# First layer's attention: scores and transposes in larger and fewer rows, group 2's factor multiplied into its probabilities

## The chip, the cores and the metric

The kernel runs on one core of a Trainium2 chip. The core has a matrix engine (TensorE, PE in the profile; its weight loads are listed as PEld), VectorE (DVE), ScalarE (ACT), GpSimd (POOL) and SyncE (SP), which mostly issues transfers. Matrix products land in PSUM, eight banks of 512 float32 columns by 128 partitions; VectorE and ScalarE read them from there. The metric is the device time of one execution in microseconds.

## What is computed

A decoder trunk of two layers over a residual stream of 512 positions by 1024 features. The change concerns the attention of the first layer, cut here to what matters:

```python
A_GROUPS = ((128, 1), (512, 4), (2048, 16))      # (window, dilation), four heads of 64 each

def dilated_mixer(xn, w_qkv, w_o, cos, sin):
    q, k, v = jnp.split(xn @ w_qkv, 3, axis=-1)   # q, k get a partial rotation
    for g, (window, r) in enumerate(A_GROUPS):
        # positions gathered by dilation r, banded causal attention in each class
        o, lse = banded_attention(gather(q), gather(k), gather(v), window // r)
        outs.append(o)
        lses.append(lse)
    alpha = jax.nn.softmax(jnp.stack(lses, axis=0), axis=0)      # weight of each group
    o = jnp.concatenate([outs[g] * alpha[g][..., None] for g in range(3)], axis=2)
    return o.reshape(B, T, A_WIDTH) @ w_o
```

The weight alpha of a group depends on the softmax denominators of all three groups, so it is known only when the last group's scores are done. After the attention come the output product with w_o, a normalisation, a feed-forward part, and the second layer.

## The kernel before

The order of all instructions is written out by hand; each engine works through its own queue in that order, and the framework adds the waits between engines. Matrix products that need precision are made as three products of high and low halves (`mm3`, L283 to L285), so every weight is first copied to a high half on ScalarE (L60, L64) and its low half made on VectorE (L78, L82). `W.get()` hands out weights and keeps some pieces ahead.

The first layer's attention is laid around three wide projections, each a call of `wide_proj`: queries and keys of group 1, those of group 2 (both `qk_ps`), and the values of groups 1 and 2 (`v_ps`). Group 0's projections come before. A `wide_proj` holds four PSUM banks, one for each block of 128 positions, through four steps; a step is 24 matmuls on TensorE. After each step it runs a list of small work (a "row" in the text) and then one step of the generator `down0`, which prepares sums of the feed-forward's weights: loads and stores on SP's queue and four subtractions on VectorE (`down_sums`, L586 to L589). `sums` is another such generator. The four lists of a call are given to it in `between`.

The small work for group g and block b:

- `qk_transpose` (L1109, `qkT_ps`): four transposes on TensorE into one bank, copied out by VectorE (L1112).
- `scores` (L1134 for group 0, L1136 for the others, `s_ps`): for each half of the heads, hh = 0 and 1, two products. The two halves use the upper and the lower 64 rows of the array, and each half has a bank of its own. In groups 1 and 2 a block's scores for two heads fill half a bank. `softmax` then reads each head's scores from PSUM on VectorE (L1119, with a second record that reads the accumulator) and exponentiates on ScalarE (L1120).
- `p_transpose` (L1156, `pT_ps`): the probabilities transposed on TensorE, copied out by ScalarE (L1158). Group 0 has two banks of them for a block, the others one.
- `factors` (L1180 to L1191): the weights alpha, with the softmax denominators in them, as a chain of small VectorE instructions and one ScalarE exponential, spread to 64 columns a head as `fac`, by VectorE for group 0 and POOL for the others.

After the third projection come, for each group and pair of heads `pr`: `pv` (L1205, L1208, `o_ps`), the product of probabilities and values, copied to SBUF by ScalarE (L1211, L1213; groups 1 and 2 back into the order of positions on the way); `weigh` (L1221, `f_ps`), the factors transposed by four transposes on TensorE and multiplied onto it by VectorE (L1223); `combine` (L1229, L1230), high and low halves of the result. Group 2's `combine` runs in `late`, a hook between the second and the third block of the output product (`Proj.finish`), together with transposes of the convolution's columns (`cv_ps`, L566) and of gains (`g_ps`, L1414). The output product (`acc`) opens two banks for each of its four blocks.

PSUM banks, and buffers of the pool `t2` (eight of 2 KB a partition, which hold probabilities, `ow` and the convolution's rows among others), are given out again when their last reader in program order is through.

Of the kernel before, what the change touches and what calls it, by code (L numbers as in the profile page):

```python
# [9 lines left out]
F32 = mybir.dt.float32  # L10
# [3 lines left out]
ALU = mybir.AluOpType  # L14
# [103 lines left out]
def trunk_kernel(ctx, tc, x, norm_gains, w_qkv_a, w_o_a, w_q_b, w_o_b, kv_norm, w_kvf, b_f,  # L118
                 w_up, conv_w, conv_b, w_down, rope, out):
    nc = tc.nc  # L120
    act, dve, pool, pe, sp = nc.scalar, nc.vector, nc.gpsimd, nc.tensor, nc.sync
# [8 lines left out]
    def t8(shape, dt=F32, name="t8"):  # L130
        return p8.tile(shape, dt, tag="t8", name=name)

    def t4(shape, dt=F32, name="t4"):
        return p4.tile(shape, dt, tag="t4", name=name)

    def t2(shape, dt=F32, name="t2"):
        return p2.tile(shape, dt, tag="t2", name=name)

    def bank(shape, name="bank"):
        return psp.tile(shape, F32, tag="ps", name=name)  # L140
# [81 lines left out]
    h = cst.tile([128, NB, D], F32, name="h")  # L222
# [889 lines left out]
        dve.tensor_copy(qkT[g][:, b], o)  # L1112

    P = {}

    def softmax(g, b, hd, s, mask, p):

        keep = st[:, g, b] if g else st0[:, b]
        dve.tensor_tensor_reduce(p, s, mask, -0.125, BIG, ALU.add, ALU.min, keep[:, hd:hd + 1])  # L1119
        act.activation(p, p, AF.Exp, bias=keep[:, hd:hd + 1], scale=-1.0, accum_out=keep[:, 4 + hd:5 + hd])  # L1120

    def scores(g, b):
        q = qkT[g]

        k0 = 0 if (g == 0 and b) else 1
        n = 256 if g == 0 else 128
        p = None
        for hh in range(2):
            hs_ = slice(64 * hh, 64 * hh + 64)
            o = bank([128, 2, n], name="s_ps")  # L1130
            for pr in range(2):
                if g == 0:
                    ov = o[:, pr, k0 * 128:].rearrange("p (k c) -> p k c", c=128)
                    pe.matmul(ov, q[hs_, b, pr, :], q[hs_, b - 1 + k0:b + 1, 2 + pr, :], start=True, stop=True)  # L1134
                else:
                    pe.matmul(o[:, pr, :], q[hs_, b, pr, :], q[hs_, b, 2 + pr, :], start=True, stop=True)  # L1136
            if g == 0 or hh == 0:
                p = t2([128, 512 // n, n], name="p")
                P[g, b, hh] = p
            for pr in range(2):  # L1140
                if g == 0:
                    softmax(g, b, 2 * pr + hh, o[:, pr, k0 * 128:], mask0[:, k0 * 128:], p[:, pr, k0 * 128:])
                else:
                    softmax(g, b, 2 * pr + hh, o[:, pr, :], mask0[:, 128:256] if g == 1 else mask2,
                            p[:, 2 * hh + pr, :])

    def p_transpose(g, b):
        if b == 0:
            PT[g] = [t8([128, 4, 4, 128], name=f"PT{g}_{i}") for i in range(2 if g == 0 else 1)]
        for pr in range(len(PT[g])):  # L1150
            p = P.pop((g, b, pr))
            o = bank([128, 4, 128], name="pT_ps")
            js = [0, 1, 2, 3] if (g or b) else [1, 3]
            pf = p.rearrange("p a c -> p (a c)")
            for j in js:
                pe.transpose(o[:, j, :], pf[:, j * 128:(j + 1) * 128], ident)  # L1156
            if len(js) == 4:
                act.copy(PT[g][pr][:, b], o)  # L1158
            else:
                for j in js:  # L1160
                    act.copy(PT[g][pr][:, b, j], o[:, j, :])
# [12 lines left out]
    def factors():  # L1174

        m, l = st[:, :, :, 0:4], st[:, :, :, 4:8]
        mn = sml.tile([128, 4, 4], F32, tag="f_mn", name="f_mn", bufs=1)
        f = sml.tile([128, 3, 4, 4], F32, tag="f_f", name="f_f", bufs=1)
        w = sml.tile([128, 3, 4, 4], F32, tag="f_w", name="f_w", bufs=1)
        dve.tensor_tensor(mn, m[:, 0], m[:, 1], ALU.min)  # L1180
        dve.tensor_tensor(mn, mn, m[:, 2], ALU.min)
        dve.tensor_tensor(f, mn[:, None].to_broadcast([128, 3, 4, 4]), m, ALU.subtract)
        act.activation(f, f, AF.Exp)
        dve.tensor_tensor(w, l, f, ALU.mult)
        dve.tensor_tensor(mn, w[:, 0], w[:, 1], ALU.add)
        dve.tensor_tensor(mn, mn, w[:, 2], ALU.add)
        dve.reciprocal(mn, mn)
        dve.tensor_tensor(f, f, mn[:, None].to_broadcast([128, 3, 4, 4]), ALU.mult)
        for g in range(3):
            fac[g] = t4([128, 4, 4, HD], name="fac")  # L1190
            (pool.tensor_copy if g else dve.tensor_copy)(fac[g], f[:, g, :, :, None].to_broadcast([128, 4, 4, HD]))  # L1191

    ow = {}

    def pv(g, pr):
        o = bank([128, T], name="o_ps")
        for b in range(4):
            for hh in range(2):
                hd = 2 * pr + hh
                ov = o[64 * hh:64 * hh + 64, b * 128:(b + 1) * 128]  # L1200
                vs = slice(hd * 64, hd * 64 + 64)
                if g == 0:
                    ks = [0, 1] if b else [1]
                    for k in ks:
                        pe.matmul(ov, V[g][:, b - 1 + k, vs], PT[g][hh][:, b, 2 * pr + k, :],  # L1205
                                  start=k == ks[0], stop=k == 1)
                else:
                    pe.matmul(ov, V[g][:, b, vs], PT[g][0][:, b, 2 * hh + pr, :], start=True, stop=True)  # L1208
        ow[g, pr] = t = t2([128, T], name="ow")
        if g == 0:  # L1210
            act.copy(t, o)  # L1211
        else:
            act.copy(t.rearrange("p (l r) -> p r l", r=4), o.rearrange("p (r l) -> p r l", r=4))  # L1213

    OT = {}

    def weigh(g, pr):

        fb = bank([128, 4, 128], name="f_ps")
        for r in range(4):  # L1220
            pe.transpose(fb[:, r, :], fac[g][:, r, 2 * pr:2 * pr + 2, :].rearrange("p h d -> p (h d)"), ident)  # L1221
        t = ow[g, pr].rearrange("p (l r) -> p r l", r=4)
        dve.tensor_tensor(t, t, fb, ALU.mult)  # L1223

    def combine(g, pr):
        t = ow.pop((g, pr))
        if pr == 0:
            OT[g] = t8([128, 2, 2, T], F32R, name=f"OT{g}")
        act.copy(OT[g][:, 0, pr, :], t)  # L1229
        dve.tensor_tensor(OT[g][:, 1, pr, :], t, OT[g][:, 0, pr, :].bitcast(F32), ALU.subtract)  # L1230

    def v_proj0(between):
        banks = []
# [20 lines left out]
    L = later  # L1254
# [86 lines left out]
    sums = down_sums([(1, 6), (1, 7)], in_two, sp, 1, 3)  # L1341
# [18 lines left out]
    def v_post(g, b, o):  # L1360
        if b == 0:
            for i in (1, 2):
# [4 lines left out]
    down0 = down_sums([*[(0, j) for j in range(ND)], (1, 8)], in_one, sp, 1, 1)  # L1367
    v_proj0([[L(qk_transpose, 0, 0), L(qk_transpose, 0, 1), L(next, down0)],
             [L(qk_transpose, 0, 2), L(qk_transpose, 0, 3), L(scores, 0, 0), L(scores, 0, 1), L(next, sums), L(next, down0)]])
    wide_proj(1, "qk_ps", qk_post, [  # L1370
        [L(p_transpose, 0, 0)],
        [L(scores, 0, 2), L(scores, 0, 3), L(p_transpose, 0, 1), L(next, sums)],
        [L(p_transpose, 0, 2), L(next, sums)],
        [stat_out, L(p_transpose, 0, 3), L(next, sums)]])
    wide_proj(2, "qk_ps", qk_post, [
        [L(qk_transpose, 1, 0), L(qk_transpose, 1, 1), L(next, sums)],
        [L(qk_transpose, 1, 2), L(scores, 1, 0), L(scores, 1, 1)],
        [L(qk_transpose, 1, 3), L(p_transpose, 1, 0)],
        [L(scores, 1, 2), L(scores, 1, 3), L(p_transpose, 1, 1), stat_in]])
    W.ahead = 3  # L1380
    wide_proj(1, "v_ps", v_post, [
        [L(qk_transpose, 2, 0), L(qk_transpose, 2, 1), L(p_transpose, 1, 2)],
        [L(qk_transpose, 2, 2), L(qk_transpose, 2, 3), L(scores, 2, 0), L(scores, 2, 1), L(p_transpose, 1, 3)],
        [L(scores, 2, 2), L(scores, 2, 3), L(p_transpose, 2, 0)],
        [factors, L(p_transpose, 2, 1), L(p_transpose, 2, 2), L(p_transpose, 2, 3)]])
    for g in range(2):
        for pr in range(2):
            pv(g, pr)
    weigh(0, 0)
    weigh(0, 1)  # L1390
    combine(0, 0)
    pv(2, 0)
    pv(2, 1)
    weigh(1, 0)
    combine(0, 1)
    weigh(1, 1)
    combine(1, 0)
    weigh(2, 0)
    combine(1, 1)
    weigh(2, 1)  # L1400

    rows = load_conv(0)
    grow = t2([16, 128], name="g_rows")
# [414 lines left out]
```

## Time and profile before

| | |
|---|---|
| median of 3 runs | 1103.44 us (1103.12 to 1103.47) |
| profiled execution | 1106.61 us, of which 1104.8 us are the span of the profile |
| first layer's attention, from the first transposes of group 0 to the output product | 41.65 to 145.34 us of the span |
| TensorE's granted clock | 0.998 of full speed |

The profile records one execution. A line of a timeline begins with an instruction's start and its duration in microseconds, then the engine, the line of the kernel, the operation, output and inputs by the program's names, and their shapes; equal neighbours are merged and counted (x8). In brackets stands how long the engine had been idle before and what released it. A line that groups instructions has, after the count, the sum of their time in microseconds and the mean of one in nanoseconds. TensorE's matmuls overlap, so what a group costs is read from start to start, not from its duration.

### The profile page before, as it was taken

How to read it: one execution, taken by the hardware profiler on the slowest of the kernel's cores; microseconds unless marked ns; L12 is line 12 of the kernel's file. 1: busy time of each engine (PE TensorE's matmuls, PEld its weight loads, DVE VectorE, ACT ScalarE, POOL GpSimd, SP SyncE). 2: the span in 40 equal slices, each digit the busy share in tenths (PEclk: the TensorE clock that was granted, in tenths of full speed). 3: DMA queues.
4: the chain of work that ended last, by engine and by line, in shares of the span. 5: the costliest groups of instructions: out<-in, count | busy, mean ns of one | idle time of the engine just before them, and what ended most of it. 6: DMA issues, size and time to landing. Idle time of an engine off the chain costs nothing.

```text
span 1104.8 us, 18091 instructions
## 1 busy us (share of the span) xinstructions
PE 1095.3 (99%) x6605; PEld 952.5 (86%) x6605; DVE 874.6 (79%) x1497; ACT 671.5 (61%) x1115; POOL 171.5 (16%) x245
## 2 busy tenths in 40 slices
PE   8999999999999999999999999999999999999997
PEld 6988889999999988888878888889899999988886
DVE  5697778887787779898587676868888788779894
ACT  6754566556665647576552488746656666647573
POOL 1723000411111211000000211100311111211000
PEclk9999999999999999999999999999999999999999
DMA  9699864378888979885445767784368888989862
GB/s 319 142 366 408 337 191 124 75 184 211 188 192 193 231 256 326 325 289 149 133 153 206 273 183 198 234 269 131 83 178 201 198 188 188 233 268 318 318 248 77
DMA packets 191554, 242.67 MB, mean 220 GB/s; under 512 B 12784, under 2 KB 138728, under 8 KB 191464
## 3 DMA queue, kind: packets, MB, share of 16 engines
q1 hardware_dynamic: 175848, 189.33, 52.8%
q0 software_dynamic: 14944, 52.18, 20.6%
q8 instruction: 52, 0.85, 0.3%
q14 instruction: 38, 0.31, 0.1%
q10 hardware_dynamic: 672, 0.00, 0.0%
HBM read 172.37 MB, written 39.73 MB: 192 GB/s over the span
## 4 chain that ended last, share of the span: by engine, by line
PE 98%; DMA 1%; DVE 0%; issue 0%; SPq 0%; ACT 0%; DVEq 0%
PE up L283 13%; PE up L284 13%; PE up L285 13%; PE acc L283 9%; PE acc L285 9%; PE acc L284 8%; PE v_ps L285 2%; PE v_ps L283 2%; PE v_ps L284 2%; PE qk_ps L284 2%; PE qk_ps L285 2%; PE qk_ps L283 2%; PE pT_ps L1659 2%; PE o_ps L1674 2%; PE s_ps L1625 2%; PE first L285 1%
## 5 line engine op out<-in xcount | busy, mean ns | idle before, releaser
L283 PE MATMUL acc<-w 128*128 128x512 f32 (+1 forms) x311 | 120.6, 388 | 0.3 <-DVE mix L332 0.3
L285 PE MATMUL acc<-w 128*128 128x512 f32 (+1 forms) x311 | 120.4, 387 | 0.0
L284 PE MATMUL acc<-w 128*128 128x512 f32 (+1 forms) x267 | 103.2, 387 | 0.0
L283 PE MATMUL up<-xsh,w 128*128 128x256 f32 x352 | 99.6, 283 | 0.0
L284 PE MATMUL up<-xsl,w 128*128 128x256 f32 x352 | 99.6, 283 | 0.0
L285 PE MATMUL up<-xsh,w 128*128 128x256 f32 x352 | 99.6, 283 | 0.0
L78 DVE TENSOR_TENSOR w<-wraw,w 128x1024 fp32r<-128x1024 f32 x62 | 82.4, 1349 | 21.7 <-ACT w L60 17.4
L620 ACT ACTIVATE bb<-up,conv 128x512 f32<-128x512 f32 x80 | 59.7, 776 | 58.4 <-DVE up L1007 47.6
L60 ACT CAST w<-wraw 128x1024 fp32r<-128x1024 f32 x81 | 83.3, 1049 | 17.0 <-PE v_ps L284 6.9
L284 PE MATMUL up<-xcl,w 128*128 128x512 f32 (+1 forms) x276 | 93.5, 339 | 0.0
L284 PE MATMUL up<-xbl,w 128*128 128x512 f32 (+1 forms) x276 | 93.5, 339 | 0.0
L285 PE MATMUL up<-xch,w 128*128 128x512 f32 (+1 forms) x276 | 93.5, 339 | 0.0
L283 PE MATMUL up<-xbh,w 128*128 128x512 f32 (+1 forms) x276 | 93.5, 339 | 0.0
L283 PE MATMUL up<-xch,w 128*128 128x512 f32 (+1 forms) x276 | 93.5, 339 | 0.0
L285 PE MATMUL up<-xbh,w 128*128 128x512 f32 (+1 forms) x276 | 93.4, 338 | 0.0
L283 PEld LDWEIGHTS acc<-w 128*128 128x128 f32 x311 | 58.4, 188 | 12.3 <-DVE mix L332 0.7
L285 PEld LDWEIGHTS acc<-w 128*128 128x128 f32 x311 | 58.4, 188 | 12.0
L283 PEld LDWEIGHTS up<-xsh,w 128*128 128x128 f32 x352 | 67.6, 192 | 0.0
L284 PEld LDWEIGHTS up<-xsl,w 128*128 128x128 f32 x352 | 67.6, 192 | 0.0
L285 PEld LDWEIGHTS up<-xsh,w 128*128 128x128 f32 x352 | 67.6, 192 | 0.0
L621 DVE SCALAR_TENSOR_TENSOR bb<-up,conv,bb 128x511 f32<-128x511 f32 x80 | 59.5, 744 | 5.8 <-ACT bb L620 5.7
L623 DVE SCALAR_TENSOR_TENSOR bb<-up,conv,bb 128x510 f32<-128x510 f32 x80 | 59.9, 749 | 2.8
(310 smaller groups left out, 3112.0 us busy)
## 6 DMA issues: line engine op xcount, KB each, us to landing
wraw<-in_w_up_dram SPq DMA_DIRECT2D x88, 512.0 KB
w<-wraw POOLq DMA_DIRECT2D x32, 512.0 KB, 6.4
dT<-dsums SPq DMA_DIRECT2D x28, 512.0 KB
w<-wsum POOLq DMA_DIRECT2D x24, 512.0 KB, 5.7
dsums<-in_w_down_dram SPq DMA_DIRECT2D x22, 512.0 KB
dsums<-in_w_down_dram SPq DMA_DIRECT2D x44, 256.0 KB
hD<-hc POOLq DMA_DIRECT2D x44, 256.0 KB, 7.1
dact<-hD SPq DMA_DIRECT2D x44, 256.0 KB
```

The source lines that it names most:

```text
L60: (copy or self.nc.scalar.copy)(pair[:, 0], raw)
L78: self.nc.vector.tensor_tensor(pair[:, 1], raw, pair[:, 0].bitcast(F32), ALU.subtract)
L283: pe.matmul(o, ah, bh, start=first, stop=False, skip_group_check=shared)
L284: pe.matmul(o, ah, bl, start=False, stop=False, skip_group_check=shared)
L285: pe.matmul(o, al, bh, start=False, stop=last, skip_group_check=shared)
L620: act.activation(bb[:, s, :], ps, AF.Identity, bias=cp[:, 3, ch:ch + 1], scale=cp[:, 2, ch:ch + 1])
L621: dve.scalar_tensor_tensor(bb[:, s, 1:], ps[:, :T - 1], cp[:, 1, ch:ch + 1], bb[:, s, 1:], ALU.mult, ALU.add)
L623: dve.scalar_tensor_tensor(bb[:, s, 2:], ps[:, :T - 2], cp[:, 0, ch:ch + 1], bb[:, s, 2:], ALU.mult, ALU.add)
L1625: pe.matmul(sc[j, i][hh][:, :nn], qT[j][own, qp, i * 128:(i + 1) * 128], k[own, kp, :nn], start=qp + kp == 0, stop=qp == 1)
L1659: pe.transpose(o[:, k0 + k, :], p[:, hh, k * 128:(k + 1) * 128], ident)
L1674: pe.matmul(o[64 * hh:64 * hh + 64, i * 128:(i + 1) * 128], Vt[hd // 8][:, k, (hd % 8) * 64:(hd % 8) * 64 + 64], pT[j, i, hh][:, k, :], st ...
```

## The change

Four things change in the first layer's attention.

1. In groups 1 and 2 the scores of blocks b and b + 1 (b even) share the two banks that one block used: one bank for each half of the heads, with block b in its first half and block b + 1 in its second.
2. The lists between the steps are cut differently: the two blocks of a pair have their transposes in one list, and the last list of each projection is left with none.
3. `factors` moves from the last list of the third projection to the one before, behind one step of `down0` (the generator has no step more, so a later one falls away). Group 2's factors are multiplied onto its probabilities before these are transposed, two blocks on VectorE and two on POOL; they are no longer spread, transposed and multiplied onto the outputs. Group 2's probabilities are transposed behind the first two `pv`.
4. Group 2's `pv` leaves its output in PSUM, and `combine` takes it from there, back into the order of positions on the way.

```diff
     P = {}
+    s_banks = {}
...
-            o = bank([128, 2, n], name="s_ps")
+            if g == 0:
+                o = bank([128, 2, n], name="s_ps")
+            else:
+                if b % 2 == 0:
+                    s_banks[hh] = bank([128, 2, 2, n], name="s_ps")
+                o = s_banks[hh][:, b % 2]
...
-        for g in range(3):
+        for b in range(4):
+            p = P[2, b, 0].rearrange("p (h r) c -> p h r c", h=2)
+            fb = f[:, 2, b].rearrange("p (r h) -> p h r", h=2)[:, :, :, None].to_broadcast([128, 2, 2, 128])
+            (pool if b >= 2 else dve).tensor_tensor(p, p, fb, ALU.mult)
+        for g in range(2):
             fac[g] = t4([128, 4, 4, HD], name="fac")
             (pool.tensor_copy if g else dve.tensor_copy)(fac[g], f[:, g, :, :, None].to_broadcast([128, 4, 4, HD]))
...
+        if g == 2:
+            ow[g, pr] = o
+            return
         ow[g, pr] = t = t2([128, T], name="ow")
...
-        act.copy(OT[g][:, 0, pr, :], t)
-        dve.tensor_tensor(OT[g][:, 1, pr, :], t, OT[g][:, 0, pr, :].bitcast(F32), ALU.subtract)
+        hi, lo = (OT[g][:, part, pr, :] for part in range(2))
+        if g == 2:
+            t = t.rearrange("p (r l) -> p r l", r=4)
+            hi, lo = (a.rearrange("p (l r) -> p r l", r=4) for a in (hi, lo))
+        act.copy(hi, t)
+        dve.tensor_tensor(lo, t, hi.bitcast(F32), ALU.subtract)
...
     wide_proj(1, "qk_ps", qk_post, [
-        [L(p_transpose, 0, 0)],
-        [L(scores, 0, 2), L(scores, 0, 3), L(p_transpose, 0, 1), L(next, sums)],
-        [L(p_transpose, 0, 2), L(next, sums)],
-        [stat_out, L(p_transpose, 0, 3), L(next, sums)]])
+        [L(p_transpose, 0, 0), L(p_transpose, 0, 1)],
+        [L(scores, 0, 2), L(scores, 0, 3), L(next, sums)],
+        [L(p_transpose, 0, 2), L(p_transpose, 0, 3), L(next, sums)],
+        [stat_out, L(next, sums)]])
     wide_proj(2, "qk_ps", qk_post, [
         [L(qk_transpose, 1, 0), L(qk_transpose, 1, 1), L(next, sums)],
-        [L(qk_transpose, 1, 2), L(scores, 1, 0), L(scores, 1, 1)],
-        [L(qk_transpose, 1, 3), L(p_transpose, 1, 0)],
-        [L(scores, 1, 2), L(scores, 1, 3), L(p_transpose, 1, 1), stat_in]])
+        [L(qk_transpose, 1, 2), L(qk_transpose, 1, 3), L(scores, 1, 0), L(scores, 1, 1)],
+        [L(p_transpose, 1, 0), L(p_transpose, 1, 1), L(scores, 1, 2), L(scores, 1, 3)],
+        [stat_in]])
     W.ahead = 3
     wide_proj(1, "v_ps", v_post, [
-        [L(qk_transpose, 2, 0), L(qk_transpose, 2, 1), L(p_transpose, 1, 2)],
-        [L(qk_transpose, 2, 2), L(qk_transpose, 2, 3), L(scores, 2, 0), L(scores, 2, 1), L(p_transpose, 1, 3)],
-        [L(scores, 2, 2), L(scores, 2, 3), L(p_transpose, 2, 0)],
-        [factors, L(p_transpose, 2, 1), L(p_transpose, 2, 2), L(p_transpose, 2, 3)]])
-    for g in range(2):
-        for pr in range(2):
-            pv(g, pr)
+        [L(p_transpose, 1, 2), L(p_transpose, 1, 3), L(qk_transpose, 2, 0), L(qk_transpose, 2, 1)],
+        [L(qk_transpose, 2, 2), L(qk_transpose, 2, 3), L(scores, 2, 0), L(scores, 2, 1)],
+        [L(scores, 2, 2), L(scores, 2, 3), L(next, down0, None), factors],
+        []])
+    pv(0, 0)
+    pv(0, 1)
+    for b in range(4):
+        p_transpose(2, b)
+    pv(1, 0)
+    pv(1, 1)
     weigh(0, 0)
     weigh(0, 1)
     combine(0, 0)
-    pv(2, 0)
-    pv(2, 1)
     weigh(1, 0)
     combine(0, 1)
     weigh(1, 1)
+    pv(2, 0)
+    pv(2, 1)
     combine(1, 0)
-    weigh(2, 0)
     combine(1, 1)
-    weigh(2, 1)
```

## The prediction

> **What bounds the kernel now.** I read the page first, then TensorE's timeline through the first layer's attention, then VectorE's beside it.
>
> ```profile
> span 1104.8 us, 18091 instructions
> PE 1095.3 (99%) x6605; PEld 952.5 (86%) x6605; DVE 874.6 (79%) x1497; ACT 671.5 (61%) x1115; POOL 171.5 (16%) x245
> ...
> PE 98%; DMA 1%; DVE 0%; issue 0%; SPq 0%; ACT 0%; DVEq 0%
> ```
>
> TensorE is busy for 99% of the span and makes 98% of the chain that ended last. A change here is worth what it takes from TensorE's queue or puts into it as waiting; work on other engines counts only where TensorE waits for it. So each row of small instructions between projections is priced by TensorE's start times (first column, us; "x8" is eight merged instructions).
>
> ```profile
> 71.19 1.03 PE L1156 MATMUL pT_ps<-ident,p 128*128 128x128 f32 x8
> 71.98 0.48 PE L283 MATMUL qk_ps<-w,xph 128*128 128x512 f32 x1
> ...
> 104.24 1.26 PE L1136 MATMUL s_ps<-qkT 64*128 64x128 f32 x16
> 105.43 0.66 PE L1156 MATMUL pT_ps<-ident,p 128*128 128x128 f32 x4
> ```
>
> Eight transposes take 71.98 - 71.19 = 0.79 us. The scores of two blocks (16 records) take 105.43 - 104.24 = 1.19 us when nothing holds them. Against these the other rows show waits:
>
> ```profile
> 64.54 1.32 PE L1156 MATMUL pT_ps<-ident,p 128*128 128x128 f32 x8
> 65.61 0.47 PE L283 MATMUL qk_ps<-w,xph 128*128 128x512 f32 x1
> ...
> 90.73 1.56 PE L1136 MATMUL s_ps<-qkT 64*128 64x128 f32 x16
> 92.22 0.50 PE L283 MATMUL qk_ps<-w,xph 128*128 128x512 f32 x1
> ...
> 119.19 1.72 PE L1136 MATMUL s_ps<-qkT 64*128 64x128 f32 x16
> 120.84 0.66 PE L1156 MATMUL pT_ps<-ident,p 128*128 128x128 f32 x4
> ...
> 126.91 1.26 PE L1136 MATMUL s_ps<-qkT 64*128 64x128 f32 x16
> 128.33 0.66 PE L1156 MATMUL pT_ps<-ident,p 128*128 128x128 f32 x4 [0.16 <-DVE st L1119]
> ```
>
> Transposes at 64.54: 1.07, so 0.28 of waiting. Scores: 1.49, 1.65 and 1.42, so 0.30, 0.46 and 0.23. The cause is banks: the projection holds four of the eight, and four for two blocks of scores with one or two for transposes in the same row ask for five or six.
>
> **What is removed.** Group 2's factors are no longer transposed: 8 of 24 transposes.
>
> ```profile
> 134.29 1.47 PE L1156 MATMUL pT_ps<-ident,p 128*128 128x128 f32 x12
> 135.69 3.33 PE L1205 MATMUL o_ps<-PT,V 128*64 128x128 f32 x56
> 138.80 1.97 PE L1208 MATMUL o_ps<-PT,V 128*64 128x128 f32 x32
> 140.70 1.09 PE L1221 MATMUL f_ps<-ident,fac 128*128 128x128 f32 x8
> ...
> 143.62 1.97 PE L1221 MATMUL f_ps<-ident,fac 128*128 128x128 f32 x16
> 145.34 0.48 PE L283 MATMUL acc<-w,OT 128*128 128x512 f32 x1
> ```
>
> Sixteen take 145.34 - 143.62 = 1.72, so eight are worth -0.86 us. The transposes of probabilities and the scores only move; their number stays. Two rows fewer interrupt the projections, but a longer row is hardly cheaper (sixteen at 0.108 each here, eight at 0.099 above): I take -0.1 (0 to -0.3). With shared banks no row asks for more than four, so the four waits go: -(0.28 + 0.30 + 0.46 + 0.23) = -1.27.
>
> **What the shared bank adds.** Blocks b and b+1 of groups 1 and 2 now share a bank for each half of the heads. TensorE writes block b+1 into a bank that VectorE still reads for block b. Before shows this case at one place, the last piece of the kernel, which writes the second half of a bank whose first half VectorE reads:
>
> ```profile
> 1097.53 0.41 DVE L332 TENSOR_TENSOR mix<-acc,gain 128x256 f32<-128x256 f32 x1
> ...
> 1098.00 0.39 PE L283 MATMUL acc<-w 128*128 128x256 f32 x1 [0.28 <-DVE mix L332]
> ```
>
> TensorE stood still until 0.06 after the read of the other half ended (1097.53 + 0.41 = 1097.94). So the order is kept by bank, not by address, and block b+1 will wait for block b's softmax reads.
>
> [...]
>
> How long the wait is, from VectorE's side:
>
> ```profile
> 118.86 1.29 DVE L1112 COPY qkT<-qkT_ps 128x512 f32<-128x512 f32 x2 [1.41 <-PE qkT_ps L1109]
> 120.07 0.28 DVE L1119 CUSTOM_DVE_ANT_0 p<-s_ps,mask 128x128 f32<-128x128 f32 x1
> ...
> 120.91 0.08 DVE L1119 DVE_READ_ACCUMULATOR2_ANT st<- 128x1 f32 x1
> ...
> 127.76 0.29 DVE L1119 CUSTOM_DVE_ANT_0 p<-s_ps,mask 128x128 f32<-128x128 f32 x1 [1.42 <-PE s_ps L1136]
> ...
> 128.61 0.08 DVE L1119 DVE_READ_ACCUMULATOR2_ANT st<- 128x1 f32 x1
> ```
>
> A block has four reads; the fourth ends with its accumulator, at 120.99 and at 128.69. From there TensorE needs 0.06 to start, and for the last half of a block the 0.64 from this row to the transposes at 120.84:
>
> ```profile
> 120.20 0.71 PE L1136 MATMUL s_ps<-qkT 64*128 64x128 f32 x4
> ```
>
> Where two copies of transposes stand ahead on VectorE (118.86), the row ends at 120.99 + 0.06 + 0.64 = 121.69, against 119.19 + 1.19 = 120.38 unheld: 1.31. Where none do, 128.69 + 0.70 = 129.39 against 126.91 + 1.19 = 128.10: 1.29. The first kind comes twice (blocks 0 and 1 of each group; group 1 now brings both copies into that row), the second twice. Together +5.2 us, bounds 0 (order by address) and 6 (VectorE behind). Queued behind the waiting score instruction is all of TensorE, first the projection; ScalarE's exponentials of block b+1 come about half a microsecond later and nothing needs them sooner.
>
> **Factors and tail.** The factors move ahead of the last 24 projection matmuls. Four products are added on the probabilities, two on VectorE (0.69, by the subtraction of that size below), two on POOL, whose rows show 5117 ns for 2048 columns, so 1.28 for 512.
>
> ```profile
> 129.46 0.69 DVE L586 TENSOR_TENSOR dsums<-dsums 128x512 f32<-128x512 f32 x1
> ...
> 132.74 1.23 DVE L78 TENSOR_TENSOR w<-wraw,w 128x1024 fp32r<-128x1024 f32 x1 [0.42 <-ACT w L60]
> 133.88 1.65 DVE L1365 TENSOR_SCALAR V<-v_ps,rt 128x256 f32<-128x256 f32 x4
> 135.45 0.17 DVE L1180 TENSOR_TENSOR f_mn<-st 128x16 f32<-128x16 f32 x1
> ...
> 137.57 0.69 DVE L1191 COPY fac<-f_f 128x1024 f32<-128x1024 f32 x1
> ```
> ```profile
> 135.39 1.10 SPq L558 DMA_DIRECT2D cv_rows<-in_conv_w_dram  x3
> ```
> ```profile
> L655 POOL TENSOR_TENSOR xsum<-xbh,xbl 128x2048 f32<-128x2048 f32 x2 | 10.2, 5117 | 52.2 <-DVE xbl L362 52.2
> ```
>
> On the old clock: softmax ends at 130.0 (0.5 later than 129.46), then four subtractions of down sums (2.8; this step stood behind the same scores before, so its subtractions and its two writes on SP keep their place), the factors' chain 137.57 - 135.45 = 2.1, products from 134.9 to 136.3 on VectorE and 137.5 on POOL. TensorE goes on with the projection at 129.39 instead of 128.75 (128.33 and four transposes), ends it 0.65 later and then has group 0's o_ps (138.80 - 135.69 = 3.11): it wants the first product near 134.29 + 0.65 + 3.11 = 138.1. Cost nothing; without that cover, or with POOL at half speed, the last block's transpose waits up to 0.9.
>
> What the factors now stand ahead of: ScalarE waits in their exponential for VectorE, and behind it are a weight's high half and V's evacuation; on VectorE the group's first factor copy (0.69), the weight's low half (1.23) and four evacuations of V (1.65) follow the products. The first V bank comes free at 136.3 + 0.7 + 1.2 + 0.4 = 138.6; TensorE wants it for the third block's transposes at 138.1 + 0.8 = 138.9. Covered, by 0.3. On SP the convolution's rows, the gains and the next weights queue behind a tile that takes a buffer of block 0's probabilities: their start moves from 135.39 to that block's transposes near 137.8, 2.4 later. They are used in or after the output projection, 7 us on. Nothing.
>
> The new hold: group 2's outputs stay in their two banks until the late combine, where before they were copied out. Four open output banks, these two and two for small transposes make eight, so the third block's output banks must wait for the combine's subtraction on VectorE.
>
> ```profile
> 141.46 2.17 DVE L1223 TENSOR_TENSOR ow<-ow,f_ps 128x512 f32<-128x512 f32 x2 [3.20 <-PE f_ps L1221]
> ...
> 152.77 1.32 DVE L1230 TENSOR_TENSOR OT<-ow,OT 128x512 fp32r<-128x512 f32 x2
> ```
> ```profile
> 151.52 0.50 PE L283 MATMUL acc<-w,OT 128*128 128x512 f32 x1
> ```
>
> After: o_ps 3.11, sixteen transposes 1.7, two o_ps 1.90 (140.70 - 138.80) bring the first factor row to 134.29 + 6.7 = 141.0, its product to 141.8 (0.76 later, as 141.46 after 140.70). VectorE's work from there to the late subtraction was 152.77 - 141.46 = 11.31, now less two of six products (2.17): it starts at 150.9 and takes 0.66 (as now) to 1.09 (reading PSUM in another order, like the products). TensorE starts the output projection at 141.0 + 1.72 + 1.90 = 144.6 and wants the bank 151.52 - 145.34 = 6.18 later, at 150.8. So it waits 0.8 to 1.2, and 0 to 0.4 more for the second bank: I take +1.4, near the strided product it resembles.
>
> **Sum:** -0.86 - 0.1 - 1.27 + 5.2 + 1.4 = +4.4 us. The profiled span of 1104.8 becomes 1109.2. Its execution took 1106.61, the runs' median 1103.44; the difference goes onto the median: 1107.8.
>
> **The rivals.** *The hold is covered* (VectorE reaches the subtraction before TensorE wants the bank; against it, VectorE shows no idle stretch there): 4.4 - 1.4 = +3.0, 1106.4. *Block b+1 does not wait* (place: the four score rows; only if the writes are ordered by address; the row at 1098.00 speaks against it): the 5.2 falls away, -0.8 with the hold, 1102.6, and -2.2 without, 1101.2, faster. It decides once less than 2.2 of the 5.2 is left without the hold. *The factor chain is late*: the last transposes wait 0.9, 1108.7. *The change does nothing*, because all of it hides: excluded by TensorE's 99%.
>
> **Chances.** Forecast 0.57, hold covered 0.15, late chain 0.08, no wait with the hold 0.08 and without 0.12. What can be told from no change is 0.2%, 2.2 us: slower 0.77 (the first three, less 0.03 for a covered hold with smaller waits), same 0.11, faster 0.12. The forecast's own range is 1105.8 to 1110.2; for 8 in 10 it is 1104.0 to 1110.6, which leaves out most of the two cases without the wait.
>
> **What would show it.** In the changed kernel each row of scores of groups 1 and 2 splits in two on TensorE, with about 1.3 us more than 1.19 and an accumulator read of softmax as the releaser; the row at 62 to 66 us and the others lose their old waits; f_ps has 16 transposes; the third block's first output matmul waits on the late subtraction. The prediction is wrong if the second block's scores start while the first block's reads still run, or if the output projection runs through.

## The result, and the profile after

The changed kernel takes 1110.41 us in the median of six runs (1109.55 to 1112.32), against 1103.45 us (1103.12 to 1103.86) for the kernel before, run along with it: a ratio of 1.0063, 95% interval 1.0052 to 1.0074. That is 7.0 us slower, where 4.4 were forecast. The profiled execution took 1111.28 us. Its span is only 4.7 us longer than that of before, because the profiled execution of before lost some 3 us at its start, ahead of the work compared here: group 0's first transposes begin at 41.65 us there and at 38.70 here.

First the page of the changed kernel: its span, the engines' busy time, and the shares of the chain that ended last.

```profile
span 1109.5 us, 18073 instructions
PE 1095.6 (99%) x6597; PEld 952.5 (86%) x6597; DVE 877.0 (79%) x1497; ACT 670.1 (60%) x1113; POOL 175.8 (16%) x246
...
PE 91%; issue 4%; DVE 2%; DMA 2%; ACT 0%; POOL 0%; DVEq 0%; POOLq 0%; ACTq 0%
```

TensorE's busy time is what it was, to 0.3 us. The time that came on is waiting, so the next view is that of the waits of TensorE, shown here for those in the attention that before lacks: who waited, for whom, the sum in us, how often, and the longest.

```profile
PE s_ps L1142 <- DVE st L1120: 2.7, 4, 0.7
PE pT_ps L1162 <- DVE V L1382: 1.6, 1, 1.6
...
PE acc L283 <- DVE OT L1247: 1.1, 1, 1.1
```

All three are waits for VectorE, at three places. The first and the last were forecast, the second was not. The same three in the timelines, first a row of scores on TensorE between two steps of the value projection:

```profile
126.42 0.39 PE L285 MATMUL v_ps<-w,xpl 128*128 128x512 f32 x1
126.73 0.72 PE L1142 MATMUL s_ps<-qkT 64*128 64x128 f32 x8
128.16 1.13 PE L1142 MATMUL s_ps<-qkT 64*128 64x128 f32 x8 [0.70 <-DVE st L1120]
129.22 0.50 PE L283 MATMUL v_ps<-w,xph 128*128 128x512 f32 x1
```

The sixteen products now stand as eight and eight with a hole between them: 129.22 - 126.73 = 2.49 us, against 1.19 for sixteen unheld. In the row of blocks 0 and 1, with the copies of transposes ahead on VectorE, TensorE goes on right after the second accumulator read of the first block:

```profile
119.86 0.08 DVE L1120 DVE_READ_ACCUMULATOR2_ANT st<- 128x1 f32 x1
...
120.28 0.08 DVE L1120 DVE_READ_ACCUMULATOR2_ANT st<- 128x1 f32 x1
```
```profile
119.99 1.13 PE L1142 MATMUL s_ps<-qkT 64*128 64x128 f32 x8 [0.71 <-DVE st L1120]
121.05 0.50 PE L283 MATMUL v_ps<-w,xph 128*128 128x512 f32 x1
```

The first half's bank is read out at 119.86 + 0.08 = 119.94, and the second block's products begin 0.05 later; the other half's bank at 120.36, and the row ends 0.69 after that. Order by bank, as forecast.

The second place is the tail, from the end of the value projection to the output product, on TensorE, VectorE and GpSimd:

```profile
134.90 3.33 PE L1215 MATMUL o_ps<-PT,V 128*64 128x128 f32 x56
138.16 1.10 PE L1162 MATMUL pT_ps<-ident,p 128*128 128x128 f32 x8
140.87 1.06 PE L1162 MATMUL pT_ps<-ident,p 128*128 128x128 f32 x8 [1.62 <-DVE V L1382]
141.87 1.97 PE L1218 MATMUL o_ps<-PT,V 128*64 128x128 f32 x32
143.77 1.97 PE L1234 MATMUL f_ps<-ident,fac 128*128 128x128 f32 x16
145.66 1.97 PE L1218 MATMUL o_ps<-PT,V 128*64 128x128 f32 x32
147.56 0.50 PE L283 MATMUL acc<-w,OT 128*128 128x512 f32 x1
```
```profile
134.77 0.69 DVE L1198 TENSOR_TENSOR p<-p,f_f 128x512 f32<-128x512 f32 x1
135.38 1.53 DVE L1198 TENSOR_TENSOR p<-p,f_f 128x512 f32<-128x512 f32 x1
136.83 1.52 DVE L1201 COPY fac<-f_f 128x1024 f32<-128x1024 f32 x1
138.28 2.05 DVE L78 TENSOR_TENSOR w<-wraw,w 128x1024 fp32r<-128x1024 f32 x1
140.26 1.65 DVE L1382 TENSOR_SCALAR V<-v_ps,rt 128x256 f32<-128x256 f32 x4
```
```profile
134.88 1.48 POOL L1198 TENSOR_TENSOR p<-p,f_f 128x512 f32<-128x512 f32 x1 [23.35 <-ACT V L1381]
136.32 1.48 POOL L1198 TENSOR_TENSOR p<-p,f_f 128x512 f32<-128x512 f32 x1
137.76 1.50 POOL L1201 COPY fac<-f_f 128x1024 f32<-128x1024 f32 x1
```

The transposes of the third block want a bank that the value projection held, and VectorE comes to empty it at 140.26, not near 138.2. The two products of each engine are listed one by one here, since their mean would hide that VectorE and GpSimd take turns. VectorE's first product starts ahead of GpSimd's and takes 0.69. Its second starts while GpSimd's first is running, takes 1.53 and ends at 136.91, which is 0.55 after GpSimd's end at 134.88 + 1.48 = 136.36. The copy of factors takes 1.52 and ends 0.55 after GpSimd's second product; the low half of a weight takes 2.05 and ends 1.08 after GpSimd's copy, which ends at 139.26. GpSimd's three instructions in turn end 0.90 after VectorE's that was running when they started. With GpSimd idle, in a run below, VectorE's three take 0.69, 0.69 and 1.23.

The third place is the third block of the output product, again TensorE and then VectorE:

```profile
153.22 0.44 PE L566 MATMUL cv_ps<-ident,cv_rows 44*128 44x44 f32 x4
153.59 0.23 PE L1432 MATMUL g_ps<-ident,g_rows 16*128 16x16 f32 x1
154.97 0.49 PE L283 MATMUL acc<-w,OT 128*128 128x512 f32 x1 [1.14 <-DVE OT L1247]
```
```profile
153.83 2.07 DVE L1247 TENSOR_TENSOR OT<-o_ps,OT 128x512 fp32r<-128x512 f32 x2
```

The first of the two subtractions takes 1.08 us by itself (the two overlap a little) and ends at 154.91; the bank is free then, and the product starts at 154.97.

What each stage costs TensorE, from its start times: from the last large matmul before the small work to the second one after it, less twice the 0.227 us that lie between the starts of two large matmuls. (The second bank of the third output block starts 155.95 - 155.53 = 0.42 after the matmul ahead of it.)

| stage | before | after | difference |
|---|---|---|---|
| rows of small work in the three projections (eleven before, nine after) | 17.70 | 21.23 | +3.53 |
| tail | 11.14 | 12.86 | +1.72 |
| ahead of the third output block | 0.74 | 1.94 | +1.20 |
| its second bank | | | +0.19 |

Together +6.6 us, of the 7.0 that the medians differ. From group 0's first transposes to the end the two profiles differ by 7.6: the profile after has two more waits of TensorE that before lacks, 0.45 for a transfer at 312.9 and 0.57 for ScalarE at 702.0, far behind the attention. They come and go between the profiles (those of the shared banks alone and of the copy to SBUF, below, have neither) and are not counted to the change.

### The profile page after: what moved, and what is told of

It reads as the page before. It is cut to its first block, busy times and chain, and to the rows that moved or that the text cites. A ratio compares the mean times of both kernels' runs of the same rounds, so it can differ in the third digit from the quotient of the medians.

```text
span 1109.5 us, 18073 instructions
## 1 busy us (share of the span) xinstructions
PE 1095.6 (99%) x6597; PEld 952.5 (86%) x6597; DVE 877.0 (79%) x1497; ACT 670.1 (60%) x1113; POOL 175.8 (16%) x246
## 4 chain that ended last, share of the span: by engine, by line
PE 91%; issue 4%; DVE 2%; DMA 2%; ACT 0%; POOL 0%; DVEq 0%; POOLq 0%; ACTq 0%
PE up L283 12%; PE up L285 12%; PE up L284 12%; PE acc L283 8%; PE acc L285 8%; PE acc L284 8%; PE v_ps L283 2%; PE v_ps L285 2%; PE v_ps L284 2%; PE qk_ps L283 2%; PE qk_ps L284 2%; PE qk_ps L285 2%; PE first L285 1%; PE first L283 1%; PE first L284 1%
```

## The experiments

Each experiment stands against its own runs of the kernel before, whose median was between 1103.52 and 1103.63 us. "Score rows" are the four rows with sixteen score products of groups 1 and 2; what they take from the first product to the work behind them is read from TensorE's start times (the figures for these rows in the expectations are up to 0.02 lower).

### The shared banks alone, in the kernel before

```diff
-            o = bank([128, 2, n], name="s_ps")
+            if g == 0:
+                o = bank([128, 2, n], name="s_ps")
+            else:
+                if b % 2 == 0:
+                    s_banks[hh] = bank([128, 2, 2, n], name="s_ps")
+                o = s_banks[hh][:, b % 2]
```

> The kernel before with the shared banks alone (lists, factors and tail as before). Theory: each of the four score rows now waits for the reads of its even block, by the same arithmetic as in the prediction: +0.9, +1.2, +0.8 and +1.1 us, together +4.0, 1107.4. Rival (the shared bank frees two banks and the old waits outweigh): 1102 to 1103.5.

1107.80 us (1107.12 to 1108.53), ratio 1.0037 (1.0024 to 1.0050): +4.3 us. The score rows take 2.37, 2.37, 2.49 and 2.48 where before they took 1.49, 1.19, 1.65 and 1.42: +3.96. Everything else stays, the tail of 11.14 included. TensorE's timeline of this kernel shows the changed kernel's hole, with no other part of the change present:

```profile
126.93 0.72 PE L1142 MATMUL s_ps<-qkT 64*128 64x128 f32 x8
128.35 1.13 PE L1142 MATMUL s_ps<-qkT 64*128 64x128 f32 x8 [0.70 <-DVE st L1120]
129.41 0.66 PE L1162 MATMUL pT_ps<-ident,p 128*128 128x128 f32 x4
```

So the sharing is what holds the rows, and the largest of the three costs.

### The changed kernel with a bank of its own for each block and half

```diff
-            if g == 0:
-                o = bank([128, 2, n], name="s_ps")
-            else:
-                if b % 2 == 0:
-                    s_banks[hh] = bank([128, 2, 2, n], name="s_ps")
-                o = s_banks[hh][:, b % 2]
+            o = bank([128, 2, n], name="s_ps")
```

> The changed kernel with a bank for each block and half of the heads again, as before the change; lists, factors and tail stay. Theory (the shared bank makes block b+1's scores wait for block b's reads): in the changed kernel's trace the four score rows of groups 1 and 2 take 2.48, 2.35, 2.48 and 2.46 us from first score to next work; with own banks the two rows without copies ahead fall to about 1.2 to 1.3 and the two with copies ahead to about 1.65, as at 119.19 before the change, since six banks are asked for there. Together -4.0 us, 1106.4. Rival (the longer rows themselves cost it, through what they queue on VectorE): the rows keep 2.3 to 2.5 us and the time stays at 1110.4.

1108.95 us (1106.84 to 1109.43), ratio 1.0042 (1.0027 to 1.0057). The score rows fell to 1.65, 1.44, 1.66 and 1.19, 3.9 us less in all, and yet the time fell by only 1.5, where 4.0 were expected: a miss. TensorE's timeline shows where 0.7 of the rest went:

```profile
137.68 1.06 PE L1157 MATMUL pT_ps<-ident,p 128*128 128x128 f32 x8 [2.33 <-DVE V L1377]
```

TensorE is at the transposes earlier, but VectorE's chain has not come earlier by as much: the wait there grew from 1.62 to 2.33. The other part is in the section on the hardware.

### The changed kernel with all scores of a pair of blocks issued before the first is read

```diff
-                    softmax(g, b, 2 * pr + hh, o[:, pr, :], mask0[:, 128:256] if g == 1 else mask2,
-                            p[:, 2 * hh + pr, :])
+                    s_reads.append((g, b, 2 * pr + hh, o[:, pr, :], mask0[:, 128:256] if g == 1 else mask2,
+                                    p[:, 2 * hh + pr, :]))
+        if b % 2:
+            while s_reads:
+                softmax(*s_reads.pop(0))
```

> The changed kernel with the bank still shared, but all score products of a pair of blocks are issued before the first read of the pair. Theory (the wait is for reads of the other half of the bank): nothing on TensorE waits any more, each of the four rows falls to about 1.2 us from first score to next work, together -5.1 us, 1105.3; softmax starts up to 0.5 us later, behind the whole pair, and nobody waits for it. Rival (a bank holding two blocks is slow in itself, or the rows are too long): no change, 1110.4. A second rival (softmax now comes late for the factors): the four rows fall, but the transposes of group 2's probabilities wait 0.5 us more.

1109.30 us (1109.04 to 1109.42), ratio 1.0048 (1.0033 to 1.0063): a clear miss, as 1105.3 was expected. The rows did what was expected, with the banks still shared:

```profile
123.04 1.26 PE L1142 MATMUL s_ps<-qkT 64*128 64x128 f32 x16
124.24 0.50 PE L283 MATMUL v_ps<-w,xph 128*128 128x512 f32 x1
...
137.03 1.94 PE L1165 MATMUL pT_ps<-ident,p 128*128 128x128 f32 x8 [2.76 <-DVE V L1385]
```

Sixteen products in 1.20, and 5.1 us less over the four rows. The wait in the tail rose to 2.76, and the tail took 15.55 instead of 12.86. So the tail was bound by VectorE's chain, and whatever TensorE gained ahead of it was in part paid back there. The tail had to be settled before the rows could pay.

### The changed kernel with group 2's values moved out of PSUM by ScalarE

```diff
-        dve.tensor_scalar(V[2][:, b, :], o[:, 256:512], factor(2, b), None, ALU.mult)
+        act.activation(V[2][:, b, :], o[:, 256:512], AF.Identity, scale=factor(2, b))
```

> The changed kernel with group 2's values moved out of PSUM by ScalarE instead of VectorE. Theory (the third block's transposes of group 2 wait 1.7 us for a bank of the value projection, because VectorE is late with that copy behind factors and products): ScalarE is done with all eight copies about 3 us sooner, the wait goes, -1.7 us, 1108.7. Rival (they wait for POOL's product on the third block's probabilities): no change, 1110.4. If VectorE's slower copies and subtractions come from POOL working beside it, they stay as slow as they are (1.5 us for the factor copy, 2.05 for the weight's low half).

1108.21 us (1107.47 to 1110.63), ratio 1.0038 (1.0024 to 1.0053): 2.2 us less than the changed kernel. The wait is gone, the sixteen transposes run as one and the tail takes 11.05:

```profile
138.03 1.97 PE L1162 MATMUL pT_ps<-ident,p 128*128 128x128 f32 x16
```

The tail's cost hung on VectorE being the one that empties the bank, and on nothing further down. That VectorE was late is so far explained by GpSimd only in argument; the next two runs test it.

### All four products on VectorE

```diff
-            (pool if b >= 2 else dve).tensor_tensor(p, p, fb, ALU.mult)
+            dve.tensor_tensor(p, p, fb, ALU.mult)
```

> The changed kernel with all four products of group 2's probabilities on VectorE, so that POOL has only its factor copy. Theory (POOL's products beside it slow VectorE: 1.07 us for a product, 1.52 for the factor copy, 2.05 for a weight's low half, where 0.69, 0.69 and 1.23 stand without): each product takes about 0.7, the low half 1.2 to 1.3, and only what runs beside POOL's copy stays slow; VectorE's work up to the first value copy is 4 x 0.7 + 1.5 + 1.2 = 5.5 us as against 2.14 + 1.52 + 2.05 = 5.7, so the time stays within 0.5 of 1110.4. Rival (the products are slow in themselves, by their repeated factor operand): 1.07 each, 0.9 us more on VectorE, and the sixteen transposes wait that much longer, 1111.3.

1110.72 us (1109.35 to 1111.99), ratio 1.0064 (1.0050 to 1.0078). VectorE has two products more and is still not later with the values. Its timeline:

```profile
134.82 3.33 DVE L1198 TENSOR_TENSOR p<-p,f_f 128x512 f32<-128x512 f32 x4
138.08 0.68 DVE L1201 COPY fac<-f_f 128x1024 f32<-128x1024 f32 x1
138.68 1.21 DVE L78 TENSOR_TENSOR w<-wraw,w 128x1024 fp32r<-128x1024 f32 x1
139.81 1.65 DVE L1382 TENSOR_SCALAR V<-v_ps,rt 128x256 f32<-128x256 f32 x4
```

GpSimd has only its copy of factors here, done by 136.4. Of VectorE's four products only the second, which starts beside that copy, is long (1.52); the others take 0.68 to 0.69, and its copy and low half take 0.68 and 1.21 again. So the products are not slow in themselves. Handing two products to GpSimd gave VectorE nothing: it was 0.45 later at the values (140.26 against 139.81).

### GpSimd idle

```diff
-        for b in range(4):
+        for b in range(2):
...
-            (pool.tensor_copy if g else dve.tensor_copy)(fac[g], f[:, g, :, :, None].to_broadcast([128, 4, 4, HD]))
+            (act.copy if g else dve.tensor_copy)(fac[g], f[:, g, :, :, None].to_broadcast([128, 4, 4, HD]))
```

> The changed kernel with GpSimd idle beside the factors: the products of blocks 2 and 3 of group 2 are left out, and group 1's factors are spread by ScalarE. Contention theory: with nothing on GpSimd, VectorE's two products take 0.69 each, the copy of group 0's factors 0.69 and the low half 1.23, so 2.4 us less than the 1.07 x 2, 1.52 and 2.05 of the changed kernel; the values of the third block's bank are out by 138.3 of its clock and the transposes need it at 139.0: the wait of 1.6 goes, the tail takes 11.0 to 11.3 us, 1108.6. Rival (the chain is late because the factors and products stand there at all, not because GpSimd slows them): VectorE keeps 2.14, 1.52 and 2.05, the wait of 1.6 stays, 1110.4. Second rival: ScalarE's extra copy of about 1 us delays its half of the values, and the wait stays with ScalarE as its releaser, 1109.5.

1109.12 us (1108.30 to 1111.64), ratio 1.0053 (1.0038 to 1.0068). This kernel leaves out the products of blocks 2 and 3. In time this run alone does not separate the theories, as its range spans them; its timelines do. VectorE does the very instructions that it does in the changed kernel, then TensorE:

```profile
134.68 1.29 DVE L1198 TENSOR_TENSOR p<-p,f_f 128x512 f32<-128x512 f32 x2
135.89 0.69 DVE L1201 COPY fac<-f_f 128x1024 f32<-128x1024 f32 x1
136.70 1.23 DVE L78 TENSOR_TENSOR w<-wraw,w 128x1024 fp32r<-128x1024 f32 x1
137.84 1.65 DVE L1382 TENSOR_SCALAR V<-v_ps,rt 128x256 f32<-128x256 f32 x4
```
```profile
138.09 1.97 PE L1162 MATMUL pT_ps<-ident,p 128*128 128x128 f32 x16
```

The durations forecast are back to a few hundredths (each product is 0.69 by itself), VectorE empties the bank at 137.84 instead of 140.26, the wait is gone, and the tail takes 11.05. That is what the contention theory said, and what neither rival did.

### Group 2's outputs copied to SBUF, as before

```diff
-        if g == 2:
-            ow[g, pr] = o
-            return
...
-        if g == 2:
-            t = t.rearrange("p (r l) -> p r l", r=4)
-            hi, lo = (a.rearrange("p (l r) -> p r l", r=4) for a in (hi, lo))
```

> The changed kernel with group 2's outputs copied to SBUF by ScalarE as before the change, nothing else. Theory (the third block of the output product waits for the late combine to free the banks): the wait of 1.2 us before the third block and the 0.2 at its second bank go, -1.4, 1109.0. Rival (what is late there is VectorE as a whole, so another wait takes its place): within 0.4 of 1110.4.

1108.51 us (1108.29 to 1108.74), ratio 1.0044 (1.0030 to 1.0058): 1.9 us less than the changed kernel. The time ahead of the third output block is back at 0.74 and the tail unchanged at 12.88. The third block starts without a wait:

```profile
153.71 0.50 PE L283 MATMUL acc<-w,OT 128*128 128x512 f32 x1
```

No bank of TensorE's hangs on VectorE's late subtraction any more: TensorE starts 0.16 us behind the transpose of gains at 153.55. Leaving the outputs in PSUM costs its hold, and that hold does not hang on the tail.

### Two cures, and three

The moved values and the copy to SBUF together, with the shared banks as in the change:

> The changed kernel with ScalarE moving group 2's values out of PSUM and with group 2's outputs copied to SBUF as before: only the four waits of the shared banks are left. If the three costs are separate, what is left is the shared bank alone: 1110.4 less 1.8 (tail) less 1.2 to 1.9 (third block) is 1106.7 to 1107.4, tail 11.05, third block 0.74, score rows unchanged at 2.35 to 2.48 for sixteen products. Rival (freeing one wait moves it to the next): above 1108.

1106.54 us (1106.04 to 1108.73), ratio 1.0029 (1.0017 to 1.0040): 3.9 us less than the changed kernel, against 2.2 and 1.9 for each alone. The costs are separate; what is left is the shared banks, with score rows unchanged (2.37 to 2.49).

The moved values and the reordered scores together:

> Both edits on the changed kernel: all score products of a pair ahead of its reads, and group 2's values moved out of PSUM by ScalarE. Theory (the rows' 5.1 us do come free, but in the run with the reads behind the pair TensorE then waited longer for VectorE's copies out of the value banks, 5.72 us for the sixteen transposes instead of 3.72): with that wait gone the two savings add up, -5.1 - 1.8 = -6.9 us, 1103.5, and the tail from the last value matmul to the output product is 11 us as with ScalarE's copies alone. Rival (the tail is held by the factor chain as a whole, products included): the sixteen transposes keep about 3 us and the time stays near 1106.

1103.59 us (1102.51 to 1105.21), ratio 1.0002 (0.9993 to 1.0011). What the reordering did not show alone, it shows here: 1108.21 - 1103.59 = 4.6 us, with the tail at 11.05.

All three:

> The changed kernel with three edits: score products of a pair ahead of its reads, group 2's values moved by ScalarE, and group 2's outputs copied to SBUF by ScalarE as before the change. Theory (each wait is separate): -5.1 - 1.8 - 1.3 = -8.2 us against the changed kernel, 1102.2, about 1.3 under the kernel before: eight factor transposes (0.86) and the old waits (1.27) less 0.4 for longer gaps in the tail. Rival (the copies to SBUF, 1.0 us each on ScalarE, hold up the combines instead): the output product starts or its third block waits, and the time stays at 1103.5.

1101.75 us (1101.26 to 1102.45), ratio 0.9983 (0.9975 to 0.9992), faster than both kernels: 1.9 us below before and 8.7 below the change. TensorE waits nowhere in the attention.

Two of them, with own banks for the scores in the reordering's place:

> As the kernel with all three cures, but each block's scores in banks of their own instead of reordered in shared ones. Score rows as with own banks before (s-part 1.63, 1.43, 1.63, 1.18), so 1.1 to 1.3 us more than with all scores of a pair issued first: 1102.9 to 1103.1, equal to the kernel before. Rival (what matters is the tail and the hold alone): 1101.7, the same as with reordered shared banks.

1103.20 us (1102.61 to 1103.74), ratio 0.9996 (0.9987 to 1.0006). The score rows take 1.65, 1.43, 1.65 and 1.19, so 5.93 against 4.77: the rows that ask for more than four banks wait a little again. A shared bank is thus the better choice, by 1.2 us in the rows and 1.45 in the medians, once no read stands between its writes.

## Why the prediction was right, and where not

**What bounds it.** Right: TensorE's busy time did not move, and the whole loss is waiting in its queue.

**The shared bank, +5.2.** Right in mechanism and size. Four unheld rows of 1.19 are 4.76; the changed kernel's take 2.49, 2.37, 2.49 and 2.48, so 9.84: +5.1. The sharing alone and the reordering, which takes it away again, give 9.72 - 4.76 = 5.0 and -5.1. By address it would have been nothing. The one row of before from the last piece of the kernel, 0.28 us of idling, carried this term.

**Old waits, transposes, fewer rows: -1.27, -0.86, -0.1.** Near. With the shared bank they were forecast at 5.2 - 1.27 - 0.86 - 0.1 = +3.0; the rows gave +3.53, and the tail without its wait, 11.05 against 11.14, -0.1: +3.4.

**The new hold, +1.4.** Right: 1.20 + 0.19 = 1.39, with VectorE's subtraction at 1.08, as the strided 1.09 that was taken.

**Factors and tail, costed at nothing.** Here the prediction failed, at "Covered, by 0.3": the first bank of values would be free at 138.6 and wanted at 138.9. (The clocks of the two profiles agree here to 0.2: the row of scores ahead starts at 126.91 and at 126.73.) TensorE was there in time; VectorE was 2 us late, and TensorE waited 1.6 and lost 1.8 (12.86 against 11.05). The chain itself was right instruction by instruction, and its start too (134.77 against 134.9). The durations were not. All were taken from rows in which GpSimd was running nothing when VectorE started, and the change itself puts two products and a copy on GpSimd beside them. The row of before for the copy of factors, 0.69 at 137.57, already showed the turns: GpSimd's copy started 0.03 later, and it was that one which was held up.

```profile
137.60 1.56 POOL L1191 COPY fac<-f_f 128x1024 f32<-128x1024 f32 x1 [26.43 <-DMA cv_rows<-in_conv_w_dram]
```

GpSimd's next copy of the same size, with VectorE idle, took 1.04. In the changed kernel it is VectorE that starts second three times. The excess is (1.53 - 0.69) + (1.52 - 0.69) + (2.05 - 1.23) = 2.5 us, which turns 138.6 into 141.1; measured, 140.26 + 0.47 = 140.7, as each of these records overlaps the next by 0.08. With GpSimd idle the excess and the wait were gone. Product, copy and subtraction are held up alike, with 0.69, 0.69 and 1.23 alone against 1.53, 1.52 and 2.05 behind an instruction of GpSimd; by what the two engines hold each other up, no run here shows.

The rival of the late chain named this place, with 0.9 us and a chance of 0.08, and a slower GpSimd as its cause. The mechanism was nearly the other way round: it is VectorE that is held up, and the wait is for the values and not for the products.

**Sum.** +4.4 forecast; +1.8 of the tail and +0.4 of small terms make the 6.6 that the trace shows. The medians differ by 7.0; the rest of 0.4 is within what the runs of the changed kernel scatter. The measured 1110.41 lies 0.2 above the forecast's own range of 1105.8 to 1110.2 and inside the wider one, up to 1110.6; the 1.8 of the tail, costed at nothing, is most of the 2.6 by which it misses the forecast of 1107.8.

**The other rivals.** *The hold is covered* and *block b+1 does not wait* are excluded by the waits of 1.1 and 2.7 us. That the old waits go with the shared banks is borne out: with the reads behind the pair, sixteen products take 1.19 in all four rows, while with own banks and the new lists they still take up to 0.47 too long.

## What to carry to other kernels

Before an instruction is costed at nothing because another engine covers it, price that cover with durations taken beside the work that the change itself adds, and ask which of the two engines starts first: VectorE's product took 0.69 us ahead of GpSimd's and 1.53 behind it, so that two products handed to GpSimd made VectorE later, not earlier. Half banks were shared here at no cost (1.20 us for the sixteen products of a pair) once all writes to a bank were issued ahead of its first read; with reads between them, each pair cost 1.2 to 1.3 us. And when two waits stand in a row, removing the first may only lengthen the second (here from 1.62 to 2.76 us), so try the cures together as well as one by one.

## What the runs showed of the hardware

TensorE's granted clock fell to 0.50 for a stretch of 3.4 us in some of the profiled executions, in five of them 1.3 to 1.7 us after the end of a wait of 1.06 to 1.15 us. The windows of the kernel with GpSimd idle, where TensorE waits once for 1.15 us before its third output block (columns: window, its length, busy time with counts of PE, PEld, DVE, ACT and POOL, then the granted clock, the DMA share and GB/s):

```profile
152.00:153.00 1.00, 0.00 (x0) 0.00 (x0) 1.00 (x3) 1.00 (x2) 0.00 (x0) 1.00 1.17 304
153.00:154.00 1.00, 0.90 (x3) 0.49 (x3) 1.00 (x3) 1.00 (x2) 0.00 (x0) 1.00 0.87 222
154.00:155.00 1.00, 0.97 (x4) 0.80 (x4) 1.00 (x4) 1.00 (x2) 0.00 (x0) 0.83 1.11 314
155.00:156.00 1.00, 1.00 (x4) 0.73 (x3) 1.00 (x2) 1.00 (x2) 0.00 (x0) 0.50 0.74 192
...
158.00:159.00 1.00, 1.00 (x6) 0.77 (x4) 1.00 (x2) 0.53 (x1) 0.00 (x0) 0.96 1.09 275
```

At half clock the starts of two large matmuls lie 0.43 apart instead of 0.23; by these starts, or by half of its 3.4 us, such a stretch costs an estimated 1.6 to 1.7 us. It stands in the profiles of five of the kernels that wait ahead of the third output block (with own banks, with reordered scores, where another stands in the tail, with moved values, with four products on VectorE, and with GpSimd idle), and not in the profiles of the changed kernel and of moved values with reordered scores, which wait there as well (1.14 and 1.12). None of the six without that wait, before included, shows it at that place (1.00 in their windows there). The profile of before has one at its start, with the clock at 0.50 from 11.5 to 14.9, 1.1 us after the end of a wait of 1.24; the two make up the 3 us that it lost there. The runs' scatter fits in part: 1101.26 to 1102.45 with all three cures and 1108.29 to 1108.74 with the copy to SBUF, but 1107.47 to 1110.63 with moved values alone, which has the wait. It is no proof, as moved values with the copy to SBUF, without the wait, run from 1106.04 to 1108.73. In the profiled executions the stretch is the other part of what own banks and the reordered scores did not gain. All but one of the waits that stood ahead of it here lasted 1.06 to 1.24 us; the one in the tail with reordered scores lasted 2.76, and there the clock fell at about 136.9, just before TensorE went on at 137.03. A longer wait does not bring it each time: 2.33 us in the tail with own banks and 1.62 in that of the changed kernel were followed by none. What decides in which executions it falls stays open.
